# The pooling groups of a hybrid mixer, taken in the opposite order

## The chip, the cores and the metric

The kernel runs on one core of a Trainium2 chip. Its time is the device time of one execution in microseconds (us). The kernel before was run three times: 989.91 us in the median, 987.9 to 990.07. One more execution was recorded by the hardware profiler; its profile and trace are what is read below. The engines are called PE (TensorE's matmuls; PEld are its weight loads), DVE (VectorE), ACT (ScalarE), POOL (GpSimd) and SP (SyncE, here only a queue of DMA issues).

## The reference

One decoder layer on 512 prompt tokens and 8 sample tokens (520 columns in all), with D = 1024: a half-step SwiGLU FFN, a mixer, a second FFN, a final norm. The mixer projects the normed input and hands the parts to two head groups. One is a Mamba-2 SSD scan with a causal convolution ahead of it; the other, which the change is about, is a pooling mixer over four groups of 128 channels, each with a causal window of its own:

```python
POOL_WINDOWS = (2, 4, 8, 16)
...
for gi, w in enumerate(POOL_WINDOWS):
    sl = slice(gi * POOL_GROUP_DIM, (gi + 1) * POOL_GROUP_DIM)
    start = POOL_STATE + 1 - w
    win_sum = end[..., sl] - cs[:, start:start + T, sl]
    cnt = jnp.minimum(w, pos + 1).astype(jnp.float32)
    outs.append(win_sum / cnt[None, :, None])
pooled = jnp.concatenate(outs, axis=-1) - u_new.astype(jnp.float32)
pg = pooled.reshape(b, T, N_POOL_GROUPS, POOL_GROUP_DIM)
mixed = jnp.einsum('btgc,gcd->btgd', pg, w_pool.astype(jnp.float32)).reshape(b, T, POOL_DIM)
out = mixed * pool_scale.astype(jnp.float32)
```

So each group is the mean over its last w tokens minus the token itself, times a 128 x 128 matrix, times a scale. The groups do not depend on each other. Both halves are joined and projected by `w_out`. The last 15 pooling inputs and the other states are outputs too.

## The kernel before

Activations lie with 128 channels on the partitions and the 520 tokens along the free axis, in two halves of 260 columns (`HALVES`). Matrix products are made of three passes (`mm3`: high by high, high by low, low by high parts of weights and inputs), so each weight tile is first split by a cast on ACT (L113) and a subtraction on DVE (L114).

The mixer is a list of small steps. Two strings, `CONV_PLAN` (L39) and `GATE_PLAN` (L43), give the order in which the steps are traced; a letter names the step and the digit its argument (table `stages`, L1062). The letters that matter here:

- `b`, `x`: input projection of one tile of 128 channels (48 matmuls, two PSUM banks), then the convolution (`conv`, L760). DVE empties the banks into a tile U (`evac`, L684 to L686), ACT and three operations of DVE (L770, L772) convolve, ACT applies Silu (L774).
- `p`: `pooling(g)` (L792): input projection of group g, evacuation into a tile U, then the window sum on POOL by doubling (L804): one add for w = 2, two for 4, three for 8, four for 16, each over some 650 columns. Two small operations (L808, L809) mend the first w - 1 tokens. Two copies (L810, L811) fill the state outputs `npp` and `spool`.
- `c`: `centre` of that group (L815 to L819): DVE scales the sum and subtracts the token, ACT casts the high part into `catp`, DVE makes the low part.
- `m`: `mix` of that group (L822): six matmuls against `w_pool` into two banks (pm), then ACT (L827) and DVE (L828) write `catp` again.
- `A`, `B`: the two halves of the SSD step of one chunk and one head group (`ssd_a` L922, `ssd_b` L964). `A` works on DVE and ACT for the decay products (ab, L950 to L961), and on POOL for xw (L960); `B` runs yo, pst and yd on PE, updates the state (hst, POOL L982, DVE L983) and adds the result into X (DVE, L990).
- `y`, `X`: the sample tokens' B and C, and their x times dt; `z`: the gate's projections; `e`: the state outputs (`outs_a`).

The U tiles, the convolution's A tiles and the pooling sums all come from one ring of six buffers (tag `cu`); PSUM has eight banks in the mixer (L571). The strings do not fix the order on an engine: they set priorities, and a planner that runs at compile time puts each engine's instructions in order by when it expects their inputs. That order is then fixed, with a wait on a semaphore wherever an input comes from another engine. SP issues the DMAs of weights and states in an order of its own that is planned in the same way.

Of the kernel before, what the change touches and what calls it, by code (L numbers as in the profile page):

```python
# [36 lines left out]
STATES = (0, 1, 1, 1, 2, 1, 1, 1)  # L37

CONV_PLAN = (  # L39
    "b0 b1 d0 b2 b3 x0 x1 v0 d1 x2 x3 d2 X0 p0 y0 c0 A0 p1 x4 m0 x5 B0 c1 p2 m1 A1 x6 c2 p3 A2 B1 x7 "  # L40
    "c3 X1 m2 A3 B2 e0"
)
GATE_PLAN = (  # L43
    "A4 z0 B3 z1 m3 z2 B4 z3 s2 A5 z4 s2 B5 A6 z5 s2 s2 G0 z6 A7 z7 B6 s2 o0 H0 s2 o1 B7 s2 o2 s2 G1 "
    "o3 g0 g1 H1 g2 g3"
)
LAST_PLAN = "h0 h2 h1 n0 h3 n1 n2 n3"
# [15 lines left out]
def tile_trunk_step(ctx: ExitStack, tc: tile.TileContext, ins: dict, outs: dict):  # L63
# [506 lines left out]

    ps[0] = tc.alloc_tile_pool(name="ppm", bufs=8, space=PSUM, reuse_waits="tile")  # L571
    mixer(tc, ins, outs, dict(locals()))
    f2["xg"].release()
    xa[0].release()
# [68 lines left out]
def mixer(tc, ins, outs, e):  # L643
# [30 lines left out]
    def inproj(src, name):  # L674
        wh, wl = load_unit(src, D, f"in{name}")
        bs = [bank(f"in{name}{b}") for b in range(2)]
        for b, hs in enumerate(HALVES):
            for k in range(KD):
                mm3(bs[b][:, :HB], ws(wh, k), ws(wl, k), xh[:, k, hs], xl[:, k, hs], k == 0, k == KD - 1)
        return bs  # L680

    def evac(bs, buf, off, soff, sstep):
        nb = SEQ - HB
        nc.vector.tensor_tensor(out=buf[:, off : off + HB], in0=bs[0][:, :HB], in1=r[:, :HB], op=ALU.mult)  # L684
        nc.vector.tensor_tensor(out=buf[:, off + HB : off + SEQ], in0=bs[1][:, :nb], in1=r[:, HB:SEQ], op=ALU.mult)
        nc.vector.tensor_tensor(out=buf[:, soff : soff + sstep * (NS - 1) + 1 : sstep], in0=bs[1][:, nb:HB],  # L686
                                in1=r[:, SEQ:NT], op=ALU.mult)
# [104 lines left out]
    def pooling(g):  # L792
        w = WINDOWS[g]
        bs = inproj(ins["w_in"][12 + g], f"p{g}")
        U = cv[0].tile([P, LP], F32, tag="cu", bufs=6, name=f"PU{g}")
        us = U[:, SAMPLE_P:LP].rearrange("p (b j) -> p b j", j=16)
        nc.gpsimd.memset(U[:, 0:PAST], 0.0)
        nc.gpsimd.tensor_copy(us[:, :, 0:PAST], spool[:, g])
        evac(bs, U, PAST, SAMPLE_P + PAST, 16)
        cur, step = U, 1  # L800
        while step < w:
            nxt = cv[0].tile([P, LP], F32, tag="cu", bufs=6, name=f"PW{g}_{step}")
            lo = 2 * step - 1
            nc.gpsimd.tensor_tensor(out=nxt[:, lo:LP], in0=cur[:, lo:LP], in1=cur[:, lo - step : LP - step], op=ALU.add)  # L804
            cur, step = nxt, 2 * step
        first = slice(PAST, PAST + w - 1)
        sx = slice(SAMPLE_P + PAST, LP, 16)
        nc.gpsimd.tensor_tensor(out=cur[:, first], in0=cur[:, first], in1=rcnt[:, : w - 1], op=ALU.mult)  # L808
        nc.gpsimd.tensor_tensor(out=cur[:, first], in0=cur[:, first], in1=U[:, first], op=ALU.subtract)  # L809
        nc.gpsimd.tensor_copy(npp[:, g], U[:, SEQ : SEQ + PAST])  # L810
        nc.gpsimd.tensor_copy(spool[:, g], us[:, :, 1:16])  # L811

        def centre():
            for q in (slice(PAST + w - 1, PAST + SEQ), sx):
                nc.vector.scalar_tensor_tensor(out=cur[:, q], in0=cur[:, q], scalar=1.0 / w, in1=U[:, q],  # L815
                                               op0=ALU.mult, op1=ALU.subtract)
            for q, t in ((slice(PAST, PAST + SEQ), slice(0, SEQ)), (sx, slice(SEQ, NT))):
                nc.scalar.copy(catp[:, 0, g, t], cur[:, q])
                nc.vector.tensor_tensor(out=catp[:, 1, g, t], in0=cur[:, q], in1=catp[:, 0, g, t].bitcast(F32),  # L819
                                        op=ALU.subtract)  # L820

        def mix():  # L822
            for b, hs in enumerate(HALVES):
                ps = bank(f"pm{g}{b}")
                mm3(ps[:, :HB], ws(wph, g), ws(wpo, g), catp[:, 0, g, hs], catp[:, 1, g, hs], True, True)
                sc = v("pool_scale", g)
                nc.scalar.activation(out=catp[:, 0, g, hs], in_=ps[:, :HB], func=AF.Copy, scale=sc)  # L827
                nc.vector.scalar_tensor_tensor(out=catp[:, 1, g, hs], in0=ps[:, :HB], scalar=sc,  # L828
                                               in1=catp[:, 0, g, hs].bitcast(F32), op0=ALU.mult, op1=ALU.subtract)
        return centre, mix  # L830
# [217 lines left out]
            if smp:  # L1048
                sample(*smp.pop(0))

    pooled, box = [], {}

    def ssd(c):
        return c % NC, c // NC
# [1 line left out]
    def outs_a():  # L1056
# [9 lines left out]
        "v": lambda j: pool_weights(),  # L1066
        "y": lambda j: sample_bc(),
        "X": sample_x,
        "p": lambda j: pooled.append(pooling(j)),
        "c": lambda j: pooled[j][0](),  # L1070
        "m": lambda j: pooled[j][1](),
        "s": samples,
# [111 lines left out]
```

## Time and profile before

| what | us |
|---|---|
| median of three runs | 989.91 |
| lowest, highest | 987.9, 990.07 |
| the profiled execution, its time | 989.39 |
| its span, first to last instruction | 987.5 |
| PE, DVE, ACT, POOL busy in it | 971.4, 797.8, 555.7, 89.6 |
| POOL busy between 424 and 482 | 37.84 |

The tables and chains shown below carry times from the start of the span. In a timeline row stand the start, the time taken, the engine, the line, the operation, out<-in with shapes, and in brackets the engine's idle time before it with what ended it. A row that ends in x2 or x4 is so many instructions merged. Matmuls overlap in the pipeline, so two rows of PE can overlap by some tenths.

### The profile page before, as it was taken

To read this page: it belongs to the slowest core of one execution; us is meant where nothing else is said; L and a number is where in the kernel's file an instruction comes from. 1 tells how busy PE (TensorE), PEld (TensorE's weight loads), DVE (VectorE), ACT (ScalarE), POOL (GpSimd) and SP (SyncE) were. 2 spreads that over 40 slices of the span, in tenths; PEclk is the share of its full clock that TensorE was granted. 3 is DMA by queue.
4 is the path that set the end of the run, shared out by engine and by line. 5 is a ranking of instruction groups with operands and counts; after the bars stand their busy time and mean duration, and the time that the engine had idled before them with its cause. 6 is when DMAs were issued, how large, how long until landed. Compare 5 with 4: busy or idle time off the path is not lost.

```text
span 987.5 us, 19451 instructions
## 1 busy us (share of the span) xinstructions
PE 971.4 (98%) x7868; PEld 952.7 (96%) x7868; DVE 797.8 (81%) x1288; ACT 555.7 (56%) x1019; POOL 89.6 (9%) x160
## 2 busy tenths in 40 slices
PE   8999999999999999999999999999999999999996
PEld 7999999999999999999899999999999999999995
DVE  6999656997569688789978997999967899668876
ACT  7766414664136455685668574666643566534653
POOL 0000000000000000156512000200012000120000
PEclk9999999999999999999999999999999999999998
DMA  5423322323222232262335232523346423453222
GB/s 181 167 90 103 112 87 85 129 86 129 86 87 81 91 126 88 82 199 106 124 113 188 73 134 86 151 103 129 110 122 197 150 94 121 123 180 121 93 65 88
DMA packets 42459, 115.53 MB, mean 117 GB/s; under 512 B 6456, under 2 KB 13560, under 8 KB 42368
## 3 DMA queue, kind: packets, MB, share of 16 engines
q1 hardware_dynamic: 38320, 103.52, 30.6%
q0 software_dynamic: 3504, 10.49, 4.0%
q8 instruction: 62, 1.02, 0.4%
q10 hardware_dynamic: 544, 0.26, 0.1%
q14 instruction: 29, 0.24, 0.1%
HBM read 106.91 MB, written 7.34 MB: 116 GB/s over the span
## 4 chain that ended last, share of the span: by engine, by line
PE 91%; DVE 4%; DMA 2%; ACT 1%; issue 1%; POOL 1%; DVEq 0%; ACTq 0%; SPq 0%
PE A L128 8%; PE A L124 8%; PE A L127 8%; PE dn L128 7%; PE dn L124 7%; PE dn L127 7%; PE BE L128 6%; PE BE L127 6%; PE BE L124 6%; PE P L254 4%; PE wo L124 2%; PE wo L128 2%; PE wo L127 2%; PE inz L124 2%; PE inz L128 2%; PE inz L127 2%
## 5 line engine op out<-in xcount | busy, mean ns | idle before, releaser
L127 PE MATMUL dn<-g,whi_1d 128*128 128x260 f32 x352 | 99.4, 282 | 0.0
L124 PE MATMUL dn<-g,whi_1d 128*128 128x260 f32 x352 | 99.2, 282 | 0.2 <-DVE td L414 0.2
L128 PE MATMUL dn<-g,wlo_1d 128*128 128x260 f32 x352 | 99.3, 282 | 0.0
L414 DVE SCALAR_TENSOR_TENSOR td<-dn,r_f 128x520 f32<-128x520 f32 x40 | 27.9, 699 | 72.7 <-PE dn L128 72.7
L128 PE MATMUL dn<-g,wlo_2d 128*128 128x260 f32 x256 | 72.6, 283 | 0.9 <-DVE wlo_2d L114 0.9
L127 PE MATMUL dn<-g,whi_2d 128*128 128x260 f32 x256 | 72.3, 282 | 0.0
L124 PE MATMUL dn<-g,whi_2d 128*128 128x260 f32 x256 | 72.3, 282 | 0.0
L124 PEld LDWEIGHTS dn<-g,whi_1d 128*128 128x128 f32 x352 | 66.1, 188 | 0.4 <-DVE td L414 0.4
L128 PEld LDWEIGHTS dn<-g,wlo_1d 128*128 128x128 f32 x352 | 66.3, 188 | 0.0
L127 PEld LDWEIGHTS dn<-g,whi_1d 128*128 128x128 f32 x352 | 66.2, 188 | 0.0
L344 ACT COPY ac<-A 128x260 f32<-128x260 f32 x123 | 45.6, 373 | 31.9 <-PE A L128 30.5
L113 ACT CAST whi_1d<-raw_1d 128x1024 fp32r<-128x1024 f32 (+1 forms) x24 | 23.4, 980 | 66.7 <-PE dn L127 54.1
L305 DVE TENSOR_TENSOR s<-raw 128x1024 f32<-128x1024 f32 x40 | 48.8, 1220 | 5.8 <-DMA raw<-in_w2gu 5.7
L128 PEld LDWEIGHTS dn<-g,wlo_2d 128*128 128x128 f32 x256 | 48.2, 188 | 1.1 <-DVE wlo_2d L114 1.1
L124 PEld LDWEIGHTS dn<-g,whi_2d 128*128 128x128 f32 x256 | 48.3, 189 | 0.0
L127 PEld LDWEIGHTS dn<-g,whi_2d 128*128 128x128 f32 x256 | 48.2, 188 | 0.0
L254 PE MATMUL P<-xg_f,raw 128*128 128x260 f32 x192 | 43.9, 383 | 1.7 <-DMA raw<-in_w1gu 1.7
L254 PEld LDWEIGHTS P<-xg_f,raw 128*128 128x128 f32 x192 | 35.9, 191 | 7.1 <-DMA raw<-in_w1gu 2.1
L124 PE MATMUL wo<-catg,whi_wo 128*128 128x260 f32 x128 | 37.2, 291 | 0.0
L124 PE MATMUL inz<-xh_mx,whi_inz 128*128 128x260 f32 x128 | 36.8, 287 | 0.0
L124 PE MATMUL inx<-xh_mx,whi_inx 128*128 128x260 f32 x128 | 36.4, 285 | 0.0
L128 PE MATMUL wo<-catg,wlo_wo 128*128 128x260 f32 x128 | 36.2, 283 | 0.0
(1350 smaller groups left out, 3949.5 us busy)
## 6 DMA issues: line engine op xcount, KB each, us to landing
raw<-in_w2gu SPq DMA_DIRECT2D x44, 512.0 KB, 4.5
raw<-in_w1gu SPq DMA_DIRECT2D x42, 512.0 KB, 4.4
raw_1d<-in_w1d SPq DMA_DIRECT2D x16, 512.0 KB, 4.4
raw_2d<-in_w2d SPq DMA_DIRECT2D x16, 512.0 KB, 4.4
raw_wo<-in_w_out SPq DMA_DIRECT2D x12, 512.0 KB, 4.7
ab<-scr_acs SPq DMA_DIRECT2D x8, 512.0 KB, 3.9
h<-in_state_ssm SPq DMA_DIRECT2D x16, 256.0 KB, 4.2
raw_inz<-in_w_in SPq DMA_DIRECT2D x8, 512.0 KB, 3.9
```

What stands on the lines that cost most here:

```text
L113: cast = nc.scalar.copy(h, src)
L124: first = nc.tensor.matmul(ps, whi, xhi, start=start, stop=False, **kw)
L127: nc.tensor.matmul(ps, whi, xlo, start=False, stop=False, **kw)
L128: nc.tensor.matmul(ps, wlo, xhi, start=False, stop=stop, **kw)
L254: nc.tensor.matmul(self.banks[f, u][b][:, :HB], ws(self.raw[f][:, u], j + 4 * q), xg[:, slot[q]], start=j == q == 0, stop=j == 3 and q == ...
L305: nc.vector.tensor_tensor(out=s1, in0=diag, in1=up0, op=ALU.add)
L344: nc.scalar.copy(keep, out[:, :HB])
L414: nc.vector.scalar_tensor_tensor(out=t, in0=banks[d][:, :, :HB], scalar=-0.5, in1=self.nx[3].rearrange("p (b t) -> p b t", b=2), op0=ALU.mult,
```

## The change

The order of the groups in the two plan strings is turned round: 3, 2, 1, 0 in place of 0, 1, 2, 3. The step letters stay at their places. Group 3 (window 16, four adds) now stands at the first place, right before `y0 c3 A0`, and group 0 (window 2, one add) at the last; groups 1 and 2 exchange places. Since group 3's functions are now asked for first, the list `pooled` becomes a dict with the group as key.

```diff
 CONV_PLAN = (
-    "b0 b1 d0 b2 b3 x0 x1 v0 d1 x2 x3 d2 X0 p0 y0 c0 A0 p1 x4 m0 x5 B0 c1 p2 m1 A1 x6 c2 p3 A2 B1 x7 "
-    "c3 X1 m2 A3 B2 e0"
+    "b0 b1 d0 b2 b3 x0 x1 v0 d1 x2 x3 d2 X0 p3 y0 c3 A0 p2 x4 m3 x5 B0 c2 p1 m2 A1 x6 c1 p0 A2 B1 x7 "
+    "c0 X1 m1 A3 B2 e0"
 )
 GATE_PLAN = (
-    "A4 z0 B3 z1 m3 z2 B4 z3 s2 A5 z4 s2 B5 A6 z5 s2 s2 G0 z6 A7 z7 B6 s2 o0 H0 s2 o1 B7 s2 o2 s2 G1 "
+    "A4 z0 B3 z1 m0 z2 B4 z3 s2 A5 z4 s2 B5 A6 z5 s2 s2 G0 z6 A7 z7 B6 s2 o0 H0 s2 o1 B7 s2 o2 s2 G1 "
     "o3 g0 g1 H1 g2 g3"
 )
...
-    pooled, box = [], {}
+    pooled, box = {}, {}
...
-        "p": lambda j: pooled.append(pooling(j)),
+        "p": lambda j: pooled.update({j: pooling(j)}),
```

## The prediction

> **What bounds the kernel now.** I read the busy table of the page first, then a table of windows cut by stage, then what ended PE's idle time, and last the chain of waits around the place where PE idles.
>
> ```profile
> span 987.5 us, 19451 instructions
> ...
> PE 971.4 (98%) x7868; PEld 952.7 (96%) x7868; DVE 797.8 (81%) x1288; ACT 555.7 (56%) x1019; POOL 89.6 (9%) x160
> ```
>
> PE is busy for 971.4 of 987.5 us. No change to the order of the work can gain more than the 16.1 us that are left, and only the part of them that lies in the mixer is near this edit.
>
> ```profile
> 364.00:424.00 60.00, 59.63 (x491) 58.18 (x490) 47.26 (x93) 35.70 (x55) 7.09 (x33) 1.00 0.33 110
> 424.00:482.00 58.00, 56.32 (x473) 52.83 (x472) 50.41 (x104) 40.96 (x87) 37.84 (x59) 1.00 0.45 148
> 482.00:542.00 60.00, 60.00 (x509) 56.28 (x509) 49.88 (x103) 45.43 (x125) 13.42 (x11) 1.00 0.42 140
> 542.00:600.00 58.00, 58.00 (x459) 56.14 (x459) 53.40 (x95) 34.85 (x93) 2.20 (x2) 1.00 0.30 101
> ...
> 870.00:890.00 20.00, 19.08 (x159) 18.88 (x158) 14.60 (x29) 7.77 (x17) 4.84 (x9) 1.00 0.47 145
> 940.00:987.50 47.50, 38.22 (x310) 37.28 (x308) 33.97 (x69) 20.92 (x45) 0.00 (x0) 0.93 0.21 69
> ```
>
> Columns: PE, PEld, DVE, ACT, POOL busy time in each stretch, then the granted clock. The mixer runs from about 364 to 600 us. From 482 to 600 PE never idles. The one stretch with something to win is 424 to 482, where the pooling lies: 58.00 - 56.32 = 1.68 us idle, with DVE at 50.41 of 58 and POOL at 37.84. Outside the mixer, 0.92 us lie at 870 to 890 and 9.28 us at the tail, behind no pooling work. The clock is 1.00 throughout the mixer. PE's idle time there sits in one cluster:
>
> ```profile
> 477.68 1.09 PE L976 MATMUL yd<-ab,xdt 128*64 128x128 f32 x16 [0.39 <-DVE U L684]
> 479.35 0.30 PE L925 MATMUL pb<-ident,BC 128*128 128x128 f32 x1 [0.58 <-DVE U L686]
> 480.53 0.55 PE L933 MATMUL px<-ident,X 128*128 128x128 f32 x3 [0.66 <-DVE xdt L957]
> ```
>
> 0.39 + 0.58 + 0.66 = 1.63 us, each time because DVE had not yet emptied a bank. Why DVE was late stands in the chain:
>
> ```profile
> 466.04 1.28 POOL PW L804
> ...
> 468.51 1.04 POOL xw L960
> 469.55 2.00 POOL hst L982
> ...
> 472.17 2.62 DVE X L990 x4
> ...
> 475.48 0.69 DVE ab L952
> ...
> 477.28 0.34 DVE U L684
> ```
>
> POOL runs a pooling add, then the SSD's xw and hst. DVE takes over with four updates of X and the decay products ab, and only then empties x7's bank (U, L684), which is what PE waits for.
>
> **The change part by part.** The group with window 16 has four adds on POOL, that with window 2 has one; the number of groups, adds and all other operations stays, ten adds in all. Only places change. The list that becomes a dict costs nothing on the chip.
>
> *Late place, 466 to 480 us (p3 becomes p0).* Three adds leave it. Next to them, the same operations of DVE took much longer than elsewhere:
>
> ```profile
> 472.17 2.61 DVE L990 SCALAR_TENSOR_TENSOR X<-X,h,E 128x128 f32<-128x128 f32 x4
> 475.48 1.80 DVE L952 TENSOR_SCALAR ab<-ab,tok 128x128 f32<-128x128 f32 x2 [0.70 <-ACT E L945]
> ...
> 485.05 1.13 DVE L990 SCALAR_TENSOR_TENSOR X<-X,h,E 128x128 f32<-128x128 f32 x4
> ```
>
> ```profile
> 471.49 2.62 POOL L804 TENSOR_TENSOR PW<-PW 128x652 f32<-128x652 f32 x2
> 475.45 1.55 POOL L804 TENSOR_TENSOR PW<-PW 128x640 f32<-128x640 f32 x1
> ```
>
> ```profile
> L952 DVE TENSOR_SCALAR ab<-ab,tok x32: 269/275/1640, 427.4 to 527.7; 128x128 f32<-128x128 f32 x32
> ```
>
> Four updates of X take 1.13 us at 485 with no add beside them, and 2.61 us under the adds of 471.49: 1.48 us lost. Two products ab take 1.80 us under the add of 475.45; the median of all 32 is 0.275 (the row of its line, least, median and most in ns), so 1.80 - 0.55 = 1.25 us lost. Together DVE stands 2.73 us on this chain because of the three adds that leave. The gain is not 2.73 but what PE idled: 1.63. The first add, at 466.04, stays, and with it the wait of xw and hst behind it. So this term is **-1.63 us**, its bounds 0 (the remaining add and hst set DVE's lateness by themselves) and -1.63.
>
> The Trainium skill ("SBUF — State Buffer", Who interferes with whom) says that a DVE instruction with two SBUF inputs and a GpSimd instruction that reads SBUF exclude each other, and that the one issued first keeps the shared ports for its whole length. The trace agrees in the 1.13 against 2.61 us. The rule also speaks against the change: three adds are moved, not removed, so at their new place they should take their own length from DVE again. By it DVE would be up to 3 x 1.28 = 3.84 us later there, an estimate of that page with this trace's add.
>
> *Early place, 422 to 441 us (p0 becomes p3).* Three more adds come here, and the scaling (L815, DVE), the cast (L818, ACT) and the remainder (L819, DVE) of the group wait for them. The rows of before:
>
> ```profile
> 427.50 1.35 POOL L804 TENSOR_TENSOR PW<-PU 128x654 f32<-128x654 f32 x1
> ...
> 429.47 0.20 POOL L808 TENSOR_TENSOR PW<-PW,rcnt 128x1 f32<-128x1 f32 x1
> 429.75 1.06 POOL L809 TENSOR_TENSOR PW<-PW,PU 128x1 f32<-128x1 f32 x1
> ...
> 436.36 1.79 POOL L804 TENSOR_TENSOR PW<-PU 128x654 f32<-128x654 f32 x1
> ...
> 438.34 2.27 POOL L804 TENSOR_TENSOR PW<-PW 128x652 f32<-128x652 f32 x1
> ...
> 460.39 1.27 POOL L808 TENSOR_TENSOR PW<-PW,rcnt 128x7 f32<-128x7 f32 x1
> ```
>
> ```profile
> 430.78 0.77 DVE L815 SCALAR_TENSOR_TENSOR PW<-PW,PU 128x511 f32<-128x511 f32 x2
> ...
> 436.24 0.78 DVE L819 TENSOR_TENSOR catp<-PW,catp 128x8 fp32r<-128x8 f32 x2
> ...
> 438.26 1.22 DVE L114 TENSOR_TENSOR wlo_inp<-raw_inp,whi_inp 128x1024 fp32r<-128x1024 f32 x1 [0.90 <-ACT whi_inp L113]
> 440.65 0.78 DVE L815 SCALAR_TENSOR_TENSOR PW<-PW,PU 128x509 f32<-128x509 f32 x2 [1.17 <-POOL PW L804]
> ...
> 444.35 0.42 DVE L684 TENSOR_TENSOR U<-inx,r_mx 128x260 f32<-128x260 f32 x1
> ```
>
> ```profile
> 433.89 0.71 ACT L818 CAST catp<-PW 128x8 fp32r<-128x8 f32 x2
> ```
>
> ```profile
> 436.92 0.28 PE L124 MATMUL pm<-catp,wph 128*128 128x260 f32 x1
> ```
>
> Before, L819 ended at 436.24 + 0.78 = 437.02 and PE took the first mix (pm) at 436.92 by the modelled starts, with no idle time: there is no slack at this one place. Behind this pm on PE stand x5, B0 and all that follows. Now the adds start at 427.50 as before. After the first, POOL spent 429.47 - 428.85 = 0.62 us on copies and other small work, which I keep. Least: four adds at the 1.28 of the chain's row, 0.62, and 0.20 each for L808 and L809 (the same size of tile), gives 433.6; the three steps on DVE and ACT add 0.77 + 0.71 + 0.78 = 2.26, so 435.9, in time. Most: four adds at 2.27, 0.62, 1.27 and 1.06, gives 439.5, and 441.8 with the three steps. PE's x4 ends at about 437.0, so a pm that stands right behind x4 waits between 0 and **4.8 us**. But the program's order on each engine comes from a planner: it can put pm into x5's matmuls, where it waits only by as much as POOL is later than planned. The nearest row for that is the 1.17 us by which DVE had to wait for POOL at 440.65, behind only two adds. I take it: **+1.17 us**. DVE's own 2.73 us of blocking come here too; 0.90 + 1.17 = 2.07 us of them fall into its idle time at 437 to 440, and the 0.66 that remain lie under PE's eight banks: outside the cluster PE idled 1.68 - 1.63 = 0.05 us in this whole stretch, so no bank was short there. I take 0 for them; if that cover were gone, 0.66.
>
> *Middle (p1 and p2 exchange).* One add more comes at 436 and one fewer at 453. Their mixes stand behind a whole input projection of 6 us, so an add of 2.27 us lies beside PE work: 0. The three small POOL steps and the copies to the two state outputs exchange places one for one.
>
> *DMA and queues.* Each group issues one weight load on SP whichever group it is. The two pool outputs wait on SP for the last group's copies, and z's weights stand behind them:
>
> ```profile
> 466.10 0.34 SPq L1059 DMA_DIRECT2D out_npp<-npp  x1
> 468.43 0.33 SPq L120 DMA_DIRECT2D raw_inz<-in_w_in  x1
> ```
>
> The last group is now group 0, whose copies follow its evacuation and its first add in the same way. Nothing moves: 0.
>
> **The sum.** The profiled execution took 989.39 us, 987.5 of span and 1.89 around it, 0.52 under the median of the runs shown, 989.91. 989.39 - 1.63 + 1.17 = 988.93; on the median's footing 989.91 - 0.46 = 989.45. I predict **989.4 us**.
>
> **The rivals.**
>
> *A, slower: the long group's chain comes too late at its new place.* The mechanism: PE stands at pm behind POOL's four adds, which DVE lengthens. For it: the 1.79 and 2.27 us adds at 436 to 440, and that pm began in the very instant in which L819 ended. Against it: the planner may place pm later, and the adds beside an idle DVE took only 1.28. Price: 4.8 us with nothing won back, 989.91 + 4.8 = 994.7; with half of it and the gain kept, 989.91 + 2.4 - 1.63 = 990.7. It decides once PE waits over 1.98 us there, or over 3.61 if the 1.63 are won.
>
> *B, slower by buffers.* Six buffers serve the conv and pooling tiles, and the long group takes one U and four sums. x5's evacuation (444.35) may have to wait for a buffer until L815 of the group before has run. With that group's three adds behind 439.5 at 2.27, and 1.27, 1.06 and 0.77, the release falls at 449.4, 5.1 us behind the evacuation; at the least lengths 433.6 + 3.84 + 0.40 + 0.77 = 438.6, in time. Price at most 5.1: 995.0.
>
> *C, the ports.* The moved adds each take their full 1.28 us from DVE at the new place: 3.84, less 2.07 of idle time, makes 1.77 us that PE would feel if a bank were short. 989.91 - 1.63 + 1.17 + 1.77 = 991.2, still inside the bound named under D. For it the 2.61 against 1.13 us; against it the 1.79 and 2.27 us adds, where POOL was the one that waited. This is the rule of the Trainium skill quoted above.
>
> *D, faster.* All 1.63 are won and the front gives nothing back, 988.3; that alone is inside the 0.2% (1.98 us) that a measurement of this kernel can tell from no change. It passes the bound only if a wait further on, such as the 0.92 at 870 to 890, resettles as well: 987.4.
>
> *E, no effect.* The planner hoists the short group's steps as it did before and PE's order hardly differs: 989.9.
>
> **How the numbers follow.** The forecast (989.4) has 0.25, E 0.03, C 0.09, and D without a second wait (988.3) 0.08: together 0.45 for no change. A has 0.30 and B 0.08, 0.38 for slower. D past the bound has 0.17, for faster. The likeliest case's own range goes from 988.3 (nothing given back) to 991.2 (C). For 8 in 10 the range reaches down to 987.3, just below D, and up to 994.7, the whole of A; B's last part is left out.
>
> **What would show it.** Right: no PE idle of 0.39, 0.58, 0.66 at x7's end, and L990 at 0.34 each there; four adds of group 3 from 427.5 on, at 1.3 to 2.3 us each; PE idle of about 1.2 us once before pm of group 3, released by DVE L819. Wrong: idle time at 477 to 481 that stays, with hst (2.00 us) as its cause; PE idle of 3 us or more between 436 and 455, released by L819 (A) or by DVE's U (B); or a difference of over 1 us after 600 us, where no pooling work runs.

## The result, and the profile after

The changed kernel took 995.48 us in the median of six runs (994.92 to 998.4), the kernel before 989.0 on the same chip (987.9 to 990.07): a ratio of 1.007 (95% interval 1.0055 to 1.0085), 6.5 us slower. The forecast of 989.4 and its range, up to 994.7, were both missed. The page of the profiled execution, 994.92 us long, has the span and the busy times:

```profile
span 993.2 us, 19446 instructions
...
PE 973.9 (98%) x7868; PEld 954.9 (96%) x7868; DVE 803.1 (81%) x1288; ACT 555.9 (56%) x1019; POOL 88.1 (9%) x160
```

The operations are the same; the span is 5.7 us longer. The table of windows (columns as before: PE, PEld, DVE, ACT, POOL, granted clock, DMA) shows the stretch:

```profile
424.00:482.00 58.00, 51.50 (x417) 49.44 (x417) 51.20 (x91) 35.21 (x71) 34.22 (x55) 0.94 0.42 144
...
440.00:441.00 1.00, 0.00 (x0) 0.00 (x0) 1.00 (x2) 0.28 (x1) 1.00 (x1) 0.59 0.00 0
...
446.00:447.00 1.00, 1.00 (x6) 1.00 (x6) 1.00 (x4) 0.00 (x0) 1.00 (x5) 0.50 0.00 0
447.00:448.00 1.00, 1.00 (x10) 1.00 (x9) 0.56 (x1) 0.00 (x0) 0.79 (x3) 1.00 0.78 168
```

PE's idle time in the stretch is 6.50 us where it was 1.68, and the mean clock is 0.94 where it was 1.00. The timeline of PE has all of it in one row:

```profile
435.90 0.28 PE L127 MATMUL inx<-xl_mx,whi_inx 128*128 128x260 f32 x1
436.02 0.28 PE L128 MATMUL inx<-xh_mx,wlo_inx 128*128 128x260 f32 x1
442.80 0.80 PE L124 MATMUL pm<-catp,wph 128*128 128x260 f32 x2 [6.50 <-ACT catp L818]
443.40 0.42 PE L124 MATMUL inx<-xh_mx,whi_inx 128*128 128x260 f32 x1
443.61 0.42 PE L127 MATMUL inx<-xl_mx,whi_inx 128*128 128x260 f32 x1
```

Two matmuls of group 3's mix stand right behind x4, and PE waits 6.50 us for the cast (L818) that they read. Then it runs at half clock: the last three rows of the windows have 0.59 while PE idles, 0.50 up to 447, 1.00 from there, and matmuls start 0.21 to 0.22 us apart (443.40, 443.61) instead of 0.12 (435.90, 436.02). For 4.2 us (442.8 to 447.0) that loses 4.2 x (1 - 0.12 / 0.217) = 1.9 us. The three idle times at x7's end, 1.63 us, are gone. The account: 6.50 + 1.9 - 1.63 = 6.8, against 6.5 measured. The starts of the n-th matmul in the two traces say the same: at 416 us (time of before) the changed kernel is 0.8 us ahead (from the first 42 us, where the two do the same), at 452 and 476 it is 7.7 us behind, at 501 it is 5.5 behind, and 5.6 at the end. So 8.5 us are lost at the first mix and 2.2 us won back around x7's end, 0.6 of them in no idle row.

Why was group 3 late? Its steps on POOL, in the timeline of the changed kernel:

```profile
426.55 1.27 POOL L804 TENSOR_TENSOR PW<-PU 128x654 f32<-128x654 f32 x1
...
428.17 1.27 POOL L804 TENSOR_TENSOR PW<-PW 128x652 f32<-128x652 f32 x1
431.70 1.05 POOL L960 TENSOR_TENSOR xw<-xdt,we 128x512 f32<-128x512 f32 x1 [2.26 <-DVE xdt L957]
432.70 1.27 POOL L804 TENSOR_TENSOR PW<-PW 128x648 f32<-128x648 f32 x1
...
434.09 1.62 POOL L804 TENSOR_TENSOR PW<-PW 128x640 f32<-128x640 f32 x1
...
435.94 1.19 POOL L808 TENSOR_TENSOR PW<-PW,rcnt 128x15 f32<-128x15 f32 x1
437.78 0.26 POOL L810 COPY npp<-PU 128x15 f32<-128x15 f32 x1 [0.65 <-DVE PU L685]
438.00 1.32 POOL L804 TENSOR_TENSOR PW<-PU 128x654 f32<-128x654 f32 x1
...
439.51 0.22 POOL L809 TENSOR_TENSOR PW<-PW,PU 128x15 f32<-128x15 f32 x1
```

The four adds take 5.43 us together; end to end from 426.55 they would be done at about 432. But between the second and third stands xw, which waits 2.26 us for DVE; and ahead of group 3's last small step (L809) stand group 2's copy, which waits for its evacuation, and group 2's first add. So L809 ends at 439.73. DVE, in the same time:

```profile
426.48 1.42 DVE L952 TENSOR_SCALAR ab<-ab,tok 128x128 f32<-128x128 f32 x1 [1.89 <-POOL we L939]
...
428.01 1.71 DVE L952 TENSOR_SCALAR ab<-ab,tok 128x128 f32<-128x128 f32 x3
...
431.87 3.97 DVE L952 TENSOR_SCALAR ab<-ab,tok 128x128 f32<-128x128 f32 x4
...
437.71 1.91 DVE L952 TENSOR_SCALAR ab<-ab,tok 128x128 f32<-128x128 f32 x4
439.54 1.87 DVE L815 SCALAR_TENSOR_TENSOR PW<-PW,PU 128x497 f32<-128x497 f32 x2
```

And the same twelve products in the kernel before:

```profile
427.43 0.29 DVE L952 TENSOR_SCALAR ab<-ab,tok 128x128 f32<-128x128 f32 x1 [2.06 <-POOL we L939]
...
428.82 0.80 DVE L952 TENSOR_SCALAR ab<-ab,tok 128x128 f32<-128x128 f32 x3
...
432.60 2.19 DVE L952 TENSOR_SCALAR ab<-ab,tok 128x128 f32<-128x128 f32 x8
```

Twelve products took 0.29 + 0.80 + 2.19 = 3.28 us and now take 1.42 + 1.71 + 3.97 + 1.91 = 9.01: beside an add, one lasts about as long as the add. The scaling (L815) needs only the fourth add, done at 435.71, but it is queued behind these products and starts at 439.54. So two queues end within 2 us of each other, and the cast follows on ACT:

```profile
441.50 0.20 ACT L818 CAST catp<-PW 128x8 fp32r<-128x8 f32 x1 [1.22 <-DVE PW L815]
441.61 0.62 ACT L954 ACTIVATE ab<-ab 128x512 f32<-128x512 f32 x1
442.14 0.60 ACT L818 CAST catp<-PW 128x512 fp32r<-128x512 f32 x1
```

### The profile page after: what moved, and what is told of

It reads as the page before. It is cut to its first block, busy times and chain, and to the rows that moved or that the text cites. A ratio compares the mean times of both kernels' runs of the same rounds, so it can differ in the third digit from the quotient of the medians.

```text
span 993.2 us, 19446 instructions
## 1 busy us (share of the span) xinstructions
PE 973.9 (98%) x7868; PEld 954.9 (96%) x7868; DVE 803.1 (81%) x1288; ACT 555.9 (56%) x1019; POOL 88.1 (9%) x160
## 4 chain that ended last, share of the span: by engine, by line
PE 50%; DVE 4%; DMA 1%; ACT 1%; issue 0%; POOL 0%; DVEq 0%; SPq 0%; ACTq 0%
PE A L124 4%; PE A L128 4%; PE A L127 4%; PE BE L128 3%; PE BE L127 3%; PE BE L124 3%; PE dn L128 3%; PE dn L127 3%; PE dn L124 2%; PE wo L124 2%; PE wo L128 2%; PE wo L127 2%; PE inz L124 2%; PE inz L128 2%; PE inz L127 2%; PE dh L128 1%
## 5 line engine op out<-in xcount | busy, mean ns | idle before, releaser
L127 PE MATMUL inx<-xl_mx,whi_inx 128*128 128x260 f32 x128 | 36.9, 288 | 0.0
L128 PE MATMUL inx<-xh_mx,wlo_inx 128*128 128x260 f32 x128 | 36.9, 288 | 0.0
```

Of the source, the lines that this page charges most:

```text
L127: nc.tensor.matmul(ps, whi, xlo, start=False, stop=False, **kw)
L128: nc.tensor.matmul(ps, wlo, xhi, start=False, stop=stop, **kw)
```

## The experiments

Theory Q: not group 3's own adds but the order of the queues decides. Work that has nothing to do with the group stands ahead of its last steps on DVE (products stretched by the adds) and on POOL (xw, group 2). Rivals: the adds' own length; the ports alone; the buffers. A second question is whether the adds of the late place made the 1.63 us at x7's end, as the prediction said. Each kernel was timed in five rounds. The kernel before took 988.79, 988.91 and 988.78 us beside the three sets of four.

| kernel | median us | ratio to before, 95% interval | PE idle at the first pm | at x7's end (475 to 485) |
|---|---|---|---|---|
| before | 988.8 | | 0 | 1.63 |
| changed | 995.48 | 1.0070 (1.0055 to 1.0085) | 6.50, then half clock | 0 |
| e1_mix_later | 991.55 | 1.0035 (1.0022 to 1.0047) | 0.74 + 1.17 | 0.24 + 1.45 |
| e2_idle_adds | 994.49 | 1.0058 (1.0045 to 1.0070) | 1.45 | 3.16, then half clock |
| e4_order_0321 | 992.28 | 1.0029 (1.0019 to 1.0039) | 0.18 | 2.43 |
| e6_products_behind | 993.97 | 1.0051 (1.0037 to 1.0064) | 4.91, then half clock | 0 |
| e7_pool_first | 991.49 | 1.0024 (1.0013 to 1.0034) | 2.67, then half clock | 0 |
| e8_both | 990.51 | 1.0016 (1.0007 to 1.0025) | 0.54 + 1.09 | 0 |
| e9_before_act | 991.41 | 1.0025 (1.0014 to 1.0035) | 0 | 0, but 3.08 at 489, then half clock |
| e10_c3_late | 988.83 | 1.0004 (0.9995 to 1.0013) | 0 | 0.38 + 0.66 |
| e4_order_1023 | 991.36 | 1.0026 (1.0016 to 1.0036) | 0.70 + 0.79 | 1.69 |
| e4_order_2103 | 995.24 | 1.0065 (1.0053 to 1.0078) | 4.68, then half clock | 0.31 |
| e12_before_outs_late | 994.10 | 1.0053 (1.0041 to 1.0066) | 0 | 3.32, then half clock |
| e11_before_a4_act | 988.74 | 1.0000 (0.9991 to 1.0009) | 0 | 0.19 + 0.50 |

### Taking the queues apart: e6, e7, e8

The changed kernel, with DVE's products of A1 and A2 queued behind group 3's last step:

```diff
+        with tc.issue_after(held["low"].ins) if (c, g) in ((1, 0), (2, 0)) else nullcontext():
             for q in range(ON_ACT, 8):
                 nc.vector.tensor_scalar(out=G[:, q], in0=ab[:, q], scalar1=atc[:, q : q + 1], scalar2=0.0,
```

(`held["low"]` is L819's last subtraction.)

> The reversed order with PE's order unchanged; only DVE's eight products ab of A1 and A2 are put behind the centring of group 3, ahead of which they took 3.97 + 1.91 us. Theory (DVE, blocked in these products by POOL's adds, is what made group 3 late): PE idle before the first pm falls from 6.50 to under 3 us, no stretch at half clock, 987.5 to 990.5 us. Rival (POOL's chain of four adds, xw and L809 itself ends too late): PE idle of 4 us or more remains, with a half clock behind it, 993 us or more.

Only part came: 1.6 us less idle time, from 6.50 to 4.91. The idle time, the half clock and the 993.97 us are those of the rival. The timeline of POOL in this kernel says why:

```profile
438.51 1.27 POOL L810 COPY npp<-PU 128x15 f32<-128x15 f32 x1
439.74 1.27 POOL L804 TENSOR_TENSOR PW<-PU 128x654 f32<-128x654 f32 x1
...
441.20 0.22 POOL L809 TENSOR_TENSOR PW<-PW,PU 128x15 f32<-128x15 f32 x1
```

DVE now waited for its inputs, and POOL was no earlier: L809 still ended behind group 2's copy and add, at 441.42. The second queue is a cause of its own.

The changed kernel, with POOL's order mended instead: group 3's four adds and two small steps in one piece, xw and group 2's adds behind them (`held["mended"]` is L809).

```diff
+        if g == 2:
+            hold.enter_context(tc.issue_after(held["mended"].ins))
...
+        with tc.issue_after(held["mended"].ins) if (c, g) == (0, 0) else nullcontext():
             nc.gpsimd.tensor_tensor(out=xw, in0=xdt, in1=we.unsqueeze(2).to_broadcast([P, 8, 64]), op=ALU.mult)
```

> The reversed order with POOL's order changed: group 3's four adds and the two mending operations run in one piece, with xw of A0 and all of group 2's adds and copies behind them. In the reversed order these stood in between. New theory (two queues made group 3 late, each by itself: DVE's products, blocked by the adds, and other work that stood in front of L809 on POOL): POOL's mending ends before 436.5, DVE is the last to come, PE idle before the first pm 2 to 5 us, 989.5 to 994 us. Rival (POOL's queue alone): PE idle under 1.5 us, under 989.5 us. Rival (DVE's queue alone): idle of 6 us or more as in the reversed order, 994.5 us or more.

The timelines of PE, then DVE, in this kernel (its lines stand some four later):

```profile
439.08 0.51 PE L124 MATMUL pm<-catp,wph 128*128 128x260 f32 x2 [2.67 <-ACT catp L822]
```

```profile
435.15 1.50 DVE L966 TENSOR_TENSOR ab<-ab,scm 128x1024 f32<-128x1024 f32 x1
436.58 1.83 DVE L819 SCALAR_TENSOR_TENSOR PW<-PW,PU 128x497 f32<-128x497 f32 x2
```

POOL was through with group 3 at 434.58, yet the scaling ran at 436.58, behind ab's product (L966). What is left is DVE's queue. But this edit did not leave DVE's queue as it was: with POOL's work in another order, A1's four products took 1.65 us (432.85) in place of 3.97, and A2's four came behind the scaling (440.33). Both edits together:

> POOL's order as in the run before, and DVE's products ab of A1 and A2 behind the centring of group 3 as well. New theory (the two queues together are the whole cause): PE idle before the first pm under 2.5 us, clock 1.00 all through, 987.5 to 990.5 us. Rival (the four adds are too long by themselves, whatever stands around them): idle of 4 us or more, half clock, 993 us or more.

```profile
437.85 0.51 PE L124 MATMUL pm<-catp,wph 128*128 128x260 f32 x2 [0.54 <-ACT catp L822]
440.41 0.39 PE L127 MATMUL pm<-catp,wph 128*128 128x260 f32 x1 [1.09 <-DVE catp L823]
```

The four kernels make a table of two by two: 6.50 us of idle time, 4.91 with DVE's queue mended, 2.67 with POOL's, 1.63 with both, and without the half clock. In each, the four adds begin at the same place, two pm stand right behind x4 and the ring has six buffers. In e8 the adds even take longer, 1.27 + 5.32 = 6.59 us against 5.43. So neither the adds' own length (rival) nor the buffers (B) made most of the 6.5 us; the two queues did. POOL's order brought more, but since it shortened DVE's queue too, how much each queue weighs by itself is not shown. e8 gives the time nearly back and is still 1.6 us behind the kernel before.

### The dose: e4_order_1023 and e4_order_2103

The same change with another group first: two adds (window 4) or three (window 8) at the first place, group 3 last as before. The plan strings:

```diff
-X0 p0 y0 c0 A0 p1 x4 m0 x5 B0 c1 p2 m1 A1 x6 c2 p3 A2 B1 x7 c3 X1 m2 A3 B2 e0 ... m3
+X0 p1 y0 c1 A0 p0 x4 m1 x5 B0 c0 p2 m0 A1 x6 c2 p3 A2 B1 x7 c3 X1 m2 A3 B2 e0 ... m3   (1023)
+X0 p2 y0 c2 A0 p1 x4 m2 x5 B0 c1 p0 m1 A1 x6 c0 p3 A2 B1 x7 c3 X1 m0 A3 B2 e0 ... m3   (2103)
```

> The group of window 4 first (two adds on POOL in front of the first mix instead of one), then groups 0, 2, 3; four adds at the late place as in the kernel before. Theory (what stands in front of the group's last steps on POOL and DVE counts, not its own adds alone): here nothing of the next group stands in front of the mending, only xw, so PE idles 1 to 3 us at the first mix and keeps the full clock; 989.5 to 992. Rival (only the adds of the group itself count, 1.28 us each): 1.3 us, 990. Rival (only a long group can do it): no idle time there, 988.9. At x7's end the 1.63 us stay, if four adds there or one make no difference.

> The group of window 8 first (three adds), then groups 1, 0, 3. On POOL xw stands between its adds, and group 1's copies and first add stand in front of its last small step L809, as in the changed kernel. Theory: PE idles 4 to 6 us at the first mix, nearly as long as with four adds, and runs at half clock behind it; 993 to 996. Rival (only the adds count): 2.6 us, 991.5 at most. At x7's end the 1.6 us stay, released by DVE.

PE's idle time at the first pm, by adds at the first place: 0 (one), 0.70 + 0.79 = 1.49 (two), 4.68 (three), 6.50 (four). From two adds to three it grows by 3.2 us, far more than an add. Both times lie in the expected ranges; at x7's end 2103 idled 0.31 us, where 1.6 had been expected. ACT's timeline of 2103 shows a third queue:

```profile
438.27 0.19 ACT L818 CAST catp<-PW 128x8 fp32r<-128x8 f32 x1
439.86 0.63 ACT L955 ACTIVATE ab<-ab 128x512 f32<-128x512 f32 x1 [1.41 <-DVE ab L952]
440.40 0.60 ACT L818 CAST catp<-PW 128x512 fp32r<-128x512 f32 x1
```

POOL (438.31) and DVE (437.95) were done with the group; the cast of the 512 tokens stood behind an exponential that waited 1.41 us for DVE's products. The same products, on another engine's queue.

### The adds alone, and the mix later: e2, e1, e4_order_0321

The kernel before, with three adds on an idle tile behind group 0's last small step on POOL (extra work; nothing reads it):

```diff
+        if g == 0:
+            idle = cv[0].tile([P, LP], F32, tag="idle", name="idle")
+            nc.gpsimd.memset(idle, 0.0)
+            with tc.issue_after(mended.ins):
+                for lo in (1, 3, 7):
+                    nc.gpsimd.tensor_tensor(out=idle[:, lo:LP], in0=idle[:, lo:LP], in1=idle[:, lo:LP], op=ALU.add)
```

> The kernel before, with three added POOL adds of the same size on a tile of their own behind group 0's POOL work, for which nothing waits. Theory (a POOL add beside DVE's products ab, L952 in the line numbers of before, blocks DVE and so delays group 0's L819, for which PE waits at once): the eight products that took 2.19 us take over 3 us, PE idle of 1.5 to 4 us before the first pm, 991 to 995 us. Rival (group 3's own chain of four adds is what made it late, DVE's share is small): no PE idle over 0.5 us there, 988.5 to 990.5 us.

No dependency is added, and PE still idled 1.45 us at the first pm, released by DVE. Its timeline has four of the products beside these adds:

```profile
433.73 2.68 DVE L958 TENSOR_SCALAR ab<-ab,tok 128x128 f32<-128x128 f32 x4
...
437.87 0.75 DVE L825 TENSOR_TENSOR catp<-PW,catp 128x8 fp32r<-128x8 f32 x2
```

Group 0's last step ran at 437.87 instead of 436.24. So adds that DVE does not wait for delay it: rival C's mechanism, of 1.45 us here. Most of this kernel's loss came later, as 1.13 + 1.72 + 0.31 us at x7's end and half clock from 482 on.

The changed kernel with only the mix `m3` moved behind x5 in the plan:

```diff
-A0 p2 x4 m3 x5 B0 c2
+A0 p2 x4 x5 m3 B0 c2
```

> The reversed order, but with the mix of group 3 (m3) one place later, behind x5 and not behind x4. Theory (PE's fixed order put m3's first matmuls right behind x4, 6.5 us before group 3's high part was ready, and the half clock after that idle time cost some 1.9 us more): PE idle before the first pm under 1 us, granted clock 1.00 from 424 to 482, the 1.63 us at x7's end still gone, 986.5 to 989 us. Rival (DVE is late as a whole, so PE is held up by x5's banks or by B0 instead): 3 us or more of PE idle between 436 and 460 at another place, 991 to 995 us.

At the first pm it did what was expected: 0.74 + 1.17 in place of 6.50, and full clock. At x7's end it did not. One add stands there, and DVE's operations are as short as the prediction wanted them, but PE idled 1.69 us all the same. The timelines of POOL, then DVE, at this place:

```profile
479.39 0.20 POOL L939 TENSOR_TENSOR we<-ab,tok 128x8 f32<-128x8 f32 x1 [3.12 <-DMA ab<-scr_acs]
```

```profile
477.16 1.12 DVE L990 SCALAR_TENSOR_TENSOR X<-X,h,E 128x128 f32<-128x128 f32 x4
...
479.63 1.66 DVE L952 TENSOR_SCALAR ab<-ab,tok 128x128 f32<-128x128 f32 x8 [0.41 <-POOL we L939]
481.21 0.41 DVE L685 TENSOR_TENSOR U<-inx,r_mx 128x252 f32<-128x252 f32 x1
```

L990 takes 1.12 us where it took 2.61, and then POOL's first step for A4 (we) waits 3.12 us for ab to land, and DVE's products wait for that step. The rest of x7's evacuation is queued behind the products of ab. On SP, ab's load stands behind the output of npp, which waits for POOL's copy of that tile: the copy ran at 469.44 and the load was issued at 472.90, in the kernel before at 465.88 and 469.29.

Groups 1 and 3 exchanged in the kernel before, so that four adds stand at the second place and two at the last:

```diff
-p1 x4 m0 x5 B0 c1 p2 m1 A1 x6 c2 p3 A2 B1 x7 c3 X1 m2 A3 B2 e0 ... m3
+p3 x4 m0 x5 B0 c3 p2 m3 A1 x6 c2 p1 A2 B1 x7 c1 X1 m2 A3 B2 e0 ... m1
```

> Groups in the order 0, 3, 2, 1: the short group stays at the first place, the long one stands second. Theory (only the first place has no slack; the other mixes stand a whole projection behind): no PE idle over 0.5 us between 424 and 470, and the idle time at x7's end shrinks from 1.63 to under 1 us because two adds leave that place: 987 to 989 us. Rival (the four adds and the products they delay hurt at any early place): PE idle of 2 us or more between 440 and 465, 991 us or more.

Four adds at the second place cost PE 0.18 us and nothing more up to 470: its mix stands behind a whole projection, as the prediction had said of the middle. The end missed: with two adds fewer there, x7's idle time is 1.20 + 0.85 + 0.38 = 2.43 us, more than before. These rows are from an execution of 990.0 us; six of the eight took 991.71 to 992.94, and what they lost beyond it is not shown.

### What sets x7's end: e9, e10, e11, e12

The kernel before with DVE's four products of an ab moved to ACT: for A3 and A4 (e9), for A4 alone (e11; its expectation says six, there are four).

```diff
-        for q in range(ON_ACT):
+        na = 8 if (c, g) in ((3, 0), (0, 1)) else ON_ACT
+        for q in range(na):
...
-        for q in range(ON_ACT, 8):
+        for q in range(na, 8):
```

> The kernel before in its own order, with the products ab of the two SSD steps that end at x7 (A3 and A4) wholly on ACT, eight operations fewer on DVE. Theory (PE's 1.63 us at x7's end are DVE being late there): they fall under 0.8 us, 0.5 to 1.2 us faster than the kernel before. Rival (what is late there is the chain from POOL's hst through X, which the products only follow): the idle time stays at 1.2 us or more, within 0.4 us of the kernel before.

> The kernel before with all eight products of A4's ab computed on ACT instead of six on DVE. Theory (DVE's work behind ab's landing is what makes U and xdt late at x7's end): the idle time there falls from 1.63 to below 0.8 us without a new wait of 3 us at yd, which came when A3's products moved too; 988 to 988.9. Rival: ACT gets late instead, and xdt or yd waits over 1 us: 989.5 to 991.

In e9 x7's idle time went, but PE then idled 3.08 us at 488.97 for a product that DVE makes from ACT's (L963). DVE was late there, and had itself waited 2.58 us for ACT (L827, at 480.39), whose queue now held the moved products; that ACT had become the bound is likely, but not tested. In e11 0.19 + 0.50 us are left at x7's end, with 0.25 new at 488: 0.7 us less idle time than before, and no difference in time that can be told (988.74 against 988.78). DVE's products are part of what is late there.

Then `c3` moved behind A3 in the plan (e10), and the two pool outputs issued on SP behind A4's ab (e12). For e12 the whole step `e0`, which issues four output DMAs, also had to move in the plans, from the end of the first to behind A4; its expectation speaks of the two alone:

```diff
-    "c3 X1 m2 A3 B2 e0"
+    "X1 m2 A3 c3 B2 e0"
```

> The kernel before with the centring of group 3 traced behind A3 and not ahead of it, so that DVE's 0.76 us for it no longer stand in front of xdt and yo's product, for which PE waits at 480.53. Theory: that wait (0.66 us) goes, the other two stay, 0.3 to 0.9 us faster than the kernel before. Rival (the same DVE work only changes its place): within 0.3 us.

```diff
-    "c3 X1 m2 A3 B2 e0"
+    "c3 X1 m2 A3 B2"
...
-    "A4 z0 B3 z1 ..."
+    "A4 e0 z0 B3 z1 ..."
...
+        with tc.issue_after(held["ab"].ins):
             nc.sync.dma_start(out=outs["npp"], in_=npp)
             nc.sync.dma_start(out=outs["nps"], in_=spool)
```

> The kernel before with one thing moved: the two pool outputs are issued on SP behind the load of A4's ab instead of in front of it, so that this load no longer waits for the last group's copies on POOL. Theory (x7's end is late because ab lands late): ab is issued about 1 us earlier, DVE waits less for it, and the idle time at x7's end falls from 1.63 to below 0.9 us; 988 to 988.8. Rival (the adds of group 3 beside DVE set it, as the prediction said): 1.63 stay, 988.9. Rival (ab waits for its buffer, which B1's yd frees): ab is issued no earlier, 988.9.

e10 takes 0.6 us off the idle time and nothing that can be told off the time (988.83 against 988.91). In e12 ab was issued on SP at 469.54, no earlier than the 469.29 of before, so it says nothing of ab's landing. But the planner answered with another order, and the kernel lost 5.3 us. The timeline of PE:

```profile
477.91 1.09 PE L976 MATMUL yd<-ab,xdt 128*64 128x128 f32 x16 [0.44 <-DVE U L684]
481.73 0.90 PE L933 MATMUL px<-ident,X 128*128 128x128 f32 x3 [2.25 <-DVE xdt L957]
```

and of POOL, then DVE:

```profile
471.69 4.24 POOL L804 TENSOR_TENSOR PW<-PW 128x652 f32<-128x652 f32 x3
```

```profile
472.37 3.97 DVE L990 SCALAR_TENSOR_TENSOR X<-X,h,E 128x128 f32<-128x128 f32 x4
...
479.25 1.83 DVE L952 TENSOR_SCALAR ab<-ab,tok 128x128 f32<-128x128 f32 x4
481.00 0.68 DVE L957 TENSOR_TENSOR xdt<-px,tok 128x512 f32<-128x512 f32 x1
```

POOL's last three adds run in one piece, where before two ran, then a step that waits for ab, then the third. DVE's four updates of X beside them take 3.97 us (2.61 before), so A4's products start at 477.04 (475.48 before). Eight products stand ahead of xdt in both kernels, but four of them now come behind x7's evacuation, beside POOL's work (1.83 us for four), and PE waits behind them: the mechanism of the changed kernel at another place, by moving one step of output DMAs. No kernel was measurably faster than the one before.

## Why the prediction was wrong, point by point

**Where it would happen: right.** The difference arises between 416 and 501, at the first mix and around x7's end; nothing moved after 600. PE idles between 436 and 455 before the first pm, which was named as the sign of rival A; the releaser is the cast L818, not L819.

**The step that failed: +1.17 us at the early place.** It measured 6.50 us, and 1.9 more by the clock. The prediction had the mechanism and its bound, 4.8 us, and then took 1.17 on the ground that the planner "can put pm into x5's matmuls, where it waits only by as much as POOL is later than planned". PE's rows show two pm right behind x4. The order is fixed at compile time, and POOL was later than planned by all of the delay.

The bound itself was too low, because it counted the group's own chain alone, in the wrong parts. On POOL it had L809's end 439.5 - 427.5 = 12.0 us after the first add's start; 439.73 - 426.55 = 13.18 were measured. The adds were shorter than the bound's (5.43 us for the four, against 4 x 2.27), and what filled the time was other work in the same queue: 3.31 us of xw with its wait, and group 2's copy and add. On DVE it kept 0.77 us for the scaling; that took 1.87 and stood behind products that had grown by 9.01 - 3.28 = 5.7 us. e6, e7 and e8 show that the two queues carry most of it: with both put right, 1.63 of the 6.50 us are left, and no half clock. And the bound had no term for the clock.

**DVE's blocking at the new place, taken as 0, at most 0.66: wrong.** The 2.73 us of the late place were carried over as the whole price. But other instructions stand there, twelve products of 0.27 us each beside adds of 1.27 to 1.62, and these rows show a short operation stretched to about the length of an add (3.97 us for four). PSUM's banks as cover did not matter: DVE's own queue was in the way of group 3.

**The -1.63 us: right in size, wrong in cause.** They are gone in the changed kernel, but not because three adds left. With one add there PE idled 1.69 us (e1), with two 2.43 (0321), with four 1.69 (1023) or 0.31 (2103). Apart from e9, they went where PE came late to the place by 2.67 us or more, and in e8 (1.63 late), but not in e1 (1.91 late); so the size came out by luck. What bounds it instead is, by e1's rows, the landing of A4's ab, with its products on DVE (e11). How much each has stays open, as e12 did not issue the load earlier.

**The middle, SP and DMA, taken as 0: right.** No row of PE's idle time there, none released by a DMA.

**The rivals.** A had the mechanism and 0.30; its price of 4.8 was 1.7 too small at this place (6.50), before the clock. B did not come: DVE has no idle time right before x5's evacuation (444.22 in the changed kernel), and e8 has six buffers too. C is real (e2: 1.45 us with no dependency), but as a part of A. D and E did not come.

The medians of e1, 1023 and e8 are 2.76, 2.58 and 1.60 us above the kernel before, their idle rows only 1.97, 1.55 and 0.19 us (e8's with one at 494). The 0.8 to 1.4 us between the two lie in no idle row of 0.1 us or more, and are not explained.

## What to carry to other kernels

When a longer chain moves ahead of a consumer whose place in its queue is fixed, price the whole queue in front of the chain's last step on every engine that it crosses, not the chain: list what a planner may put between its parts, and what each of those waits for. A planner that prices an operation as if it ran alone will place the consumer too early wherever two engines slow each other down, and then nothing gives way. If a stall of some 2.5 us or more is among the outcomes, add the half clock that these runs show behind it to the price.

## What the runs showed of the hardware

**Half clock after short stalls.** PE's clock fell to 0.50 for idle times of 6.50, 4.91, 4.68, 3.08 (e9) and 2.67 us (e7), and with 1.13 + 1.72 (e2) and 0.44 + 2.25 (e12) that lay a few us apart; it stayed full with 0.74 + 1.17, 0.70 + 0.79, 0.54 + 1.09 and 0.39 + 0.58 + 0.66. The windows of e12, then of e7:

```profile
480.00:481.00 1.00, 0.00 (x0) 0.00 (x0) 1.00 (x2) 1.00 (x3) 0.99 (x1) 0.95 0.48 146
481.00:482.00 1.00, 0.27 (x1) 0.27 (x2) 1.00 (x3) 1.00 (x3) 0.24 (x1) 0.50 0.16 61
...
487.00:488.00 1.00, 1.00 (x8) 1.00 (x8) 1.00 (x3) 0.00 (x0) 0.00 (x0) 0.63 0.00 0
```

```profile
439.00:440.00 1.00, 0.92 (x7) 0.92 (x8) 1.00 (x2) 1.00 (x3) 1.00 (x2) 0.95 0.00 0
...
443.00:444.00 1.00, 1.00 (x9) 1.00 (x9) 1.00 (x3) 0.76 (x2) 0.11 (x2) 0.84 0.00 0
```

A mean of 0.95 in a slice of 1 us means that the last 0.10 us ran at half. So in e12 the clock was down from 480.90 to 487.74, 6.8 us, and fell 1.4 us after the idle time began (481.73 - 2.25 = 479.48). In the changed kernel it was down from 440.18 to 447.0, again 6.8, and fell 3.9 us after the beginning (436.30). In e7 it was down from 439.90 to 443.32, 3.4 us, and fell when PE had been at work again for 0.8 us. The Trainium skill ("TensorE: Matmul & The Clock Gate", Part 1: The HAM clock gate) describes a window of about 3.4 us that runs freely, a drop after an idle one and full speed after a busy one. The lengths of one and two such windows and the different delays agree with that. But stalls of 2.67 and 2.25 us, shorter than the window, were enough, so a window need not be idle throughout; the measurement decides. Near the edge it seems to depend on the execution: 0321, with 2.43 us in three pieces, took 989.45 and 990.0 us in two runs with a mean clock of 0.996 and 0.997, and 991.71 to 992.94 in six with 0.994 or 0.995. Only one of these has a trace, so that is a reading.

**A small DVE operation beside POOL's work can take that work's time.** A product of 128 x 128 with a single tensor input, 0.27 us alone, took 3.97 / 4 = 1.0 us beside POOL operations of 1.05 to 1.62. It is not so every time: of two products that each began 0.07 us ahead of an add, the one at 427.43 before kept 0.29 us, the one at 426.48 in the changed kernel took 1.42. The section of the Trainium skill cited in the prediction ("SBUF — State Buffer", Who interferes with whom) names this operation among those that can enter a two-port mode and then shut GpSimd out, or be shut out, for a whole instruction; the rows agree with that. The prediction used it for operations with two SBUF inputs alone.
